# Rotary embedding on one core: the two table loads issued from GpSimd instead of ScalarE

## The chip, the cores and the metric

The kernel runs on one core of one Trainium2 chip. The metric is the device time in microseconds of one execution; lower is better. The profile's span (first to last instruction) is about 2 us shorter than this time.

For a program on one core a timed run is called slow when it lies over 1.5% above the fastest run of its own kernel. Ratios use fast runs only: a ratio is the mean time of one kernel's fast runs over that of the other's of the same rounds, so it is not quite the ratio of the medians quoted.

## The reference

```python
x:   (16, 512, 16, 64) float32      # batch, seq, heads, dim; 33.5 MB
cos, sin: (512, 32) float32         # 64 KB each
x1, x2 = x[..., :32], x[..., 32:]
first  = x1[..., :16] * cos[..., :16] - x1[..., 16:] * sin[..., :16]
second = x1[..., :16] * sin[..., :16] + x1[..., 16:] * cos[..., :16]
return concatenate([first, second, x2], axis=-1)
```

Only the first half of each head is rotated. All of x is read once and written once.

## The kernel before

x is cut into T = 8 tiles of 4 MB, each 128 partitions x 32 KB. A tile is loaded on SyncE's DMA queue, rotated in place on VectorE in two halves, and stored from ScalarE's DMA queue. Five tile buffers exist (`bufs=5`), so the load of tile i+5 waits for the store of tile i.

```python
x_pool  = ...tile_pool(name="xp", bufs=5)
ab_pool = ...tile_pool(name="abp", bufs=1)

stage = const_pool.tile([PB, 2, K, HF], fp32)              # PB = 64 partitions, K = 8, HF = 32
nc.scalar.dma_start(out=stage[:, 0]..., in_=cosf)          # 64 rows of 1 KB
nc.scalar.dma_start(out=stage[:, 1]..., in_=sinf)

table = const_pool.tile([P, 2, K, 2, Q], fp32)
# ... four small VectorE copies, stage -> table (64 partitions to 128) ...

for t in range(T):
    x_t = x_pool.tile([P, K, H, D], fp32)
    nc.sync.dma_start(out=x_t..., in_=xf[t])               # 4 MB, 128 rows of 32 KB
    for k0 in range(0, K, KC):                             # KC = 4: two halves
        # x1, c, s: views of this half of x_t and of the table
        nc.vector.tensor_mul(out=a_t[:], in0=x1, in1=c)
        nc.vector.tensor_mul(out=b_t[:], in0=x1, in1=s)
        nc.vector.tensor_sub(out=x1[:, :, :, 0:Q], in0=..., in1=...)
        nc.vector.tensor_add(out=x1[:, :, :, Q:HF], in0=..., in1=...)
    nc.scalar.dma_start(out=of[t], in_=x_t...)
```

Of the kernel before, what the change touches and what calls it, by code (L numbers as in the profile page):

```python
# [1 line left out]

# [4 lines left out]


@with_exitstack
def kernel(  # L10
    ctx: ExitStack,
    tc: tile.TileContext,
    x: bass.AP,
    cos: bass.AP,
    sin: bass.AP,
    out: bass.AP,
):
    nc = tc.nc
    fp32 = mybir.dt.float32
    P = 128  # L20
    B, S, H, D = x.shape
    Q = D // 4
    HF = D // 2


    K = 8
    T = B * S // (P * K)
    PB = S // K
    REP = P // PB

    xf = x.rearrange("b s h d -> (b s h d)").rearrange("(t p f) -> t p f", t=T, p=P)
    of = out.rearrange("b s h d -> (b s h d)").rearrange("(t p f) -> t p f", t=T, p=P)
    cosf = cos.rearrange("(p k) j -> p (k j)", k=K)
    sinf = sin.rearrange("(p k) j -> p (k j)", k=K)

    const_pool = ctx.enter_context(tc.tile_pool(name="const", bufs=1))
    x_pool = ctx.enter_context(tc.tile_pool(name="xp", bufs=5))
    ab_pool = ctx.enter_context(tc.tile_pool(name="abp", bufs=1))

    stage = const_pool.tile([PB, 2, K, HF], fp32)  # L40
    nc.scalar.dma_start(out=stage[:, 0].rearrange("p k j -> p (k j)"), in_=cosf)  # L41
    nc.scalar.dma_start(out=stage[:, 1].rearrange("p k j -> p (k j)"), in_=sinf)


    table = const_pool.tile([P, 2, K, 2, Q], fp32)
    for r in range(REP):
        for t in range(2):
            nc.vector.tensor_copy(  # L48
                out=table[r * PB : (r + 1) * PB, t],
                in_=stage[:, t, :, 0:Q].unsqueeze(2).to_broadcast((PB, K, 2, Q)),  # L50
            )
    C = table[:, 0].rearrange("p k c j -> p k (c j)")
    Sn = table[:, 1].rearrange("p k c j -> p k (c j)")

    KC = 4
    for t in range(T):
        x_t = x_pool.tile([P, K, H, D], fp32)
        nc.sync.dma_start(out=x_t.rearrange("p k h d -> p (k h d)"), in_=xf[t])  # L58
        for k0 in range(0, K, KC):
            x1 = x_t[:, k0 : k0 + KC, :, 0:HF]  # L60
            c = C[:, k0 : k0 + KC].unsqueeze(2).to_broadcast((P, KC, H, HF))
            s = Sn[:, k0 : k0 + KC].unsqueeze(2).to_broadcast((P, KC, H, HF))
            a_t = ab_pool.tile([P, KC, H, HF], fp32)
            b_t = ab_pool.tile([P, KC, H, HF], fp32)
            nc.vector.tensor_mul(out=a_t[:], in0=x1, in1=c)  # L65
            nc.vector.tensor_mul(out=b_t[:], in0=x1, in1=s)  # L66
            nc.vector.tensor_sub(  # L67
                out=x1[:, :, :, 0:Q], in0=a_t[:, :, :, 0:Q], in1=b_t[:, :, :, Q:HF]
            )
            nc.vector.tensor_add(  # L70
                out=x1[:, :, :, Q:HF], in0=a_t[:, :, :, Q:HF], in1=b_t[:, :, :, 0:Q]
            )
        nc.scalar.dma_start(out=of[t], in_=x_t.rearrange("p k h d -> p (k h d)"))


# [1 line left out]
_INS = ['x', 'cos', 'sin']  # L77
_OUTS = [((16, 512, 16, 64), 'float32')]


# [23 lines left out]
```

## Time and profile before

| | before |
|---|---|
| time, median of 3 runs | 162.37 us (162.19 to 162.39) |
| span of the profiled execution | 160.4 us |
| VectorE (DVE) busy | 110.8 us, 69% |
| DMA engines | full in all but the first and last slices, 419 GB/s over the span |
| first real multiply starts | 18.29 us |

The page of the kernel before. The DMA row gives the mean busy share of the 16 DMA engines in tenths, for 40 equal slices of the span. The queue lines give packets, MB and the share of the 16 engines' time. Group lines end with busy us, mean ns of one, then the idle time just before them and what ended it. Issue lines end with KB each and us from issue to landing.

```profile
DVE 110.8 (69%) x68; POOL 0.2 (0%) x4
...
DMA  7999999999999999999999999999999999999993
GB/s 253 408 400 408 392 417 490 400 408 498 400 400 474 433 392 457 457 392 449 466 392 417 490 400 408 498 400 400 476 425 400 466 441 400 449 457 400 417 482 147
...
q1 hardware_dynamic: 1152, 33.55, 49.3%
q10 hardware_dynamic: 1312, 33.69, 48.7%
...
L65 DVE TENSOR_TENSOR a_t<-x_t,table 128x2048 f32<-128x2048 f32 x16 | 36.7, 2292 | 13.6 <-DMA x_t<-in_x_dram 13.2
...
L48 DVE COPY table<-stage 64x256 f32<-64x256 f32 x4 | 1.1, 287 | 17.1 <-DMA stage<-in_cos_dram 12.2
...
stage<-in_cos_dram ACTq DMA_DIRECT2D x1, 64.0 KB, 11.4
stage<-in_sin_dram ACTq DMA_DIRECT2D x1, 64.0 KB, 16.3
```

From about 4 us on, the DMA engines never rest. q1 is SyncE's queue (x in), q10 ScalarE's (x out and the tables).

The trace also keeps every DMA packet with queue, start, duration and size; the numbers called "packet records" below are counted from those. A 32 KB row of x is one packet of 1.213 us; 16 engines at that pace move 16 x 32768 B / 1.213 us = 432 GB/s. Each engine moves 64 packets in and 64 out: 128 x 1.213 = 155.3 us, and 157.0 us with the slower early loads and the tables. The first packet starts 1.8 us into the span, the last end at 158.2 to 159.2, and the gaps on each engine sum to at most 0.4 us.

The chain of waits of the kernel before, in order of time (start us, us, what):

```profile
1.30 16.34 DMA stage<-in_sin_dram
...
18.29 2.29 DVE a_t L65
...
59.83 34.11 DMA out_dram<-x_t
...
93.99 34.21 DMA x_t<-in_x_dram
...
140.97 1.14 DVEq L99
```

The chain begins with 16 us of waiting for two 64 KB tables. The next pieces show that a load waits for a store that waits its turn in a full queue. The chain names what released what. The last store, issued at 142.1 us, had to queue behind store 6, which landed at 150.0 us (semaphore landings): 7.9 us of slack between VectorE's last result and an engine free to move it.

### The profile page before, as it was taken

The page shows a single profiled execution, that of the slowest core. Times are in us where ns is not written, and L with a number is a line of the kernel's source. Part 1 is how long each engine was busy: PE and PEld are TensorE (multiplying, and loading weights), DVE is VectorE, ACT ScalarE, POOL GpSimd, SP SyncE. Part 2 cuts the span into 40 slices and gives each one's busy share as a digit, 9 for nine tenths or more (in the row PEclk, how much of TensorE's full clock was granted, in tenths as well). Part 3 has the DMA queues.
Part 4 walks back from the last instruction along what each step waited for, and adds up shares of the span by engine and source line. Part 5 has one row for each costly group of instructions (what it writes and reads, how often), then busy time and mean ns, then how long its engine had stood idle before and what let it go on. Part 6 is the DMA issues. An engine that isn't in the chain of part 4 may idle for free.

```text
span 160.4 us, 155 instructions
## 1 busy us (share of the span) xinstructions
DVE 110.8 (69%) x68; POOL 0.2 (0%) x4
## 2 busy tenths in 40 slices
DVE  0001599999999999999998799609995099940000
POOL 0000000000000000000000000000000000000000
DMA  7999999999999999999999999999999999999993
GB/s 253 408 400 408 392 417 490 400 408 498 400 400 474 433 392 457 457 392 449 466 392 417 490 400 408 498 400 400 476 425 400 466 441 400 449 457 400 417 482 147
DMA packets 2465, 67.25 MB, mean 419 GB/s; under 512 B 288, under 2 KB 416, under 8 KB 416
## 3 DMA queue, kind: packets, MB, share of 16 engines
q1 hardware_dynamic: 1152, 33.55, 49.3%
q10 hardware_dynamic: 1312, 33.69, 48.7%
q14 instruction: 1, 0.01, 0.0%
HBM read 33.69 MB, written 33.55 MB: 419 GB/s over the span
## 4 chain that ended last, share of the span: by engine, by line
DMA 53%; DVE 30%; issue 4%; DVEq 1%; ACTq 0%; SPq 0%
DMA x_t<-in_x_dram 21%; DMA out_dram<-x_t 21%; DVE b_t L66 11%; DMA stage<-in_sin_dram 10%; DVE a_t L65 10%; DVE x_t L70 5%; DVE x_t L67 4%; DVEq L99 1%; ACTq L41 0%; DVE table L48 0%; SPq L58 0%; DVEq L65 0%
## 5 line engine op out<-in xcount | busy, mean ns | idle before, releaser
L65 DVE TENSOR_TENSOR a_t<-x_t,table 128x2048 f32<-128x2048 f32 x16 | 36.7, 2292 | 13.6 <-DMA x_t<-in_x_dram 13.2
L66 DVE TENSOR_TENSOR b_t<-x_t,table 128x2048 f32<-128x2048 f32 x16 | 36.5, 2284 | 0.0
L67 DVE TENSOR_TENSOR x_t<-a_t,b_t 128x1024 f32<-128x1024 f32 x16 | 19.6, 1226 | 0.6
L70 DVE TENSOR_TENSOR x_t<-a_t,b_t 128x1024 f32<-128x1024 f32 x16 | 19.5, 1218 | 0.0
L48 DVE COPY table<-stage 64x256 f32<-64x256 f32 x4 | 1.1, 287 | 17.1 <-DMA stage<-in_cos_dram 12.2
L88 POOL MEMSET const-bfloat16-1.0<- 128x1 bf16 x1 | 0.1, 102 | 0.0
L88 POOL MEMSET const-uint8-127<- 128x1 uint8 x1 | 0.1, 102 | 0.0
L88 POOL MEMSET const-float32-0.0<- 128x1 f32 x1 | 0.1, 99 | 0.2 <-issue 0.2
L88 POOL MEMSET const-float32-1.0<- 128x1 f32 x1 | 0.1, 99 | 0.0
## 6 DMA issues: line engine op xcount, KB each, us to landing
x_t<-in_x_dram SPq DMA_DIRECT2D x8, 4096.0 KB, 33.9
out_dram<-x_t ACTq DMA_DIRECT2D x8, 4096.0 KB, 31.3
stage<-in_cos_dram ACTq DMA_DIRECT2D x1, 64.0 KB, 11.4
stage<-in_sin_dram ACTq DMA_DIRECT2D x1, 64.0 KB, 16.3
```

What stands on the lines that cost most here:

```text
L48: nc.vector.tensor_copy(out=table[r * PB : (r + 1) * PB, t], in_=stage[:, t, :, 0:Q].unsqueeze(2).to_broadcast((PB, K, 2, Q)),)
L65: nc.vector.tensor_mul(out=a_t[:], in0=x1, in1=c)
L66: nc.vector.tensor_mul(out=b_t[:], in0=x1, in1=s)
L67: nc.vector.tensor_sub(out=x1[:, :, :, 0:Q], in0=a_t[:, :, :, 0:Q], in1=b_t[:, :, :, Q:HF])
L70: nc.vector.tensor_add(out=x1[:, :, :, Q:HF], in0=a_t[:, :, :, Q:HF], in1=b_t[:, :, :, 0:Q])
L88: nc = _bacc.Bacc("TRN2", target_bir_lowering=False, num_devices=1)
L99: with _tile.TileContext(nc) as tc:
```

## The change

The intent: in the packet records of the kernel before, each 1 KB row of a table is a packet of its own on ScalarE's queue, and an engine alternates it (46 ns) with a 32 KB x packet (1.213 us). From GpSimd's queue several rows were expected to go in one packet (the prediction says why), so the tables should land sooner, and the two other queues are left to x.

```diff
-    nc.scalar.dma_start(out=stage[:, 0].rearrange("p k j -> p (k j)"), in_=cosf)
-    nc.scalar.dma_start(out=stage[:, 1].rearrange("p k j -> p (k j)"), in_=sinf)
+    nc.gpsimd.dma_start(out=stage[:, 0].rearrange("p k j -> p (k j)"), in_=cosf)
+    nc.gpsimd.dma_start(out=stage[:, 1].rearrange("p k j -> p (k j)"), in_=sinf)
```

## The prediction

> **What bounds the kernel now.** The 16 DMA engines, start to end. In the page's 40 slices the DMA share is 9 in all but the first (7) and last (3). In the packet records a 32 KB x packet takes 1.213 us on its engine, and each engine moves 64 in and 64 out: loads 64 x 1.234 (mean), stores 64 x 1.213, table packets 8 x 0.047, together 157.0 us. The first packet starts at 1.8 us, the last end at 158.2 to 159.2, and each engine's gaps add up to at most 0.35 us. The span is 160.4. VectorE is busy 110.8 us (69%).
>
> **What the change moves.** By the instruction order, only the two table loads, from ScalarE's DMA queue to GpSimd's. The fifth x load no longer waits for cos.
>
> Today both tables come as 1 KB packets on ScalarE's queue. In the packet records each engine alternates one of them (46 ns) with one x packet (1.213 us), so ten table packets per engine (eight data, two completion) wait for about ten x packets: the first at 6.0 us; cos lands at 12.2, sin at 17.65. The Trainium skill, "DMA: Bandwidth & Descriptors" ("Queues, rings and completion order"), has the engines go round-robin between queues by packet; the trace agrees. Its section "SWDGE vs HWDGE vs iDMA" prefers packets up to 4096 B for descriptors that GpSimd writes; no run shows that yet. Four 1 KB rows would be one packet, and each table would wait for one or two x packets. Estimate: cos lands at 6 to 9 us, sin at 7 to 11.
>
> **What lies on the path.** The first multiply (18.3 us) waits for sin; x tile 0 landed at 13.6. Its start moves to about 13.2, released by x: 5 us earlier. The first store moves from 32.1 to about 27.
>
> But almost no DMA work goes away: the same bytes cross the same full engines. Stores share the engines with loads earlier, so loads come later. Sharing, a tile in and a tile out take 19.4 us. Loads run alone until 27; 5.4 tiles are left, so the last x tile lands at about 133 (128.2 before). Its 13.9 us of VectorE end at about 147 (142.1 before); store 6 lands at about 148.7 (150.0 before, by the semaphore landings). The last store still queues behind it; slack falls from 7.9 to about 2 us. Total packet time sets the end. Possible gain: some of the 1.4 us by which early x packets exceed 1.213 each (0.6 of it at 8 to 16 us, among table packets). Possible loss: a gap under 1 us before the last store, or GpSimd start and end costs.
>
> **Prediction: 162.1 us, 161.2 to 163.2.** Faster by over 2%: 0.02; within: 0.95; slower: 0.03.
>
> **What would show each step right or wrong.**
> - Queues: a third carries 0.13 MB; tables land under 10 us after issue (11.4 and 16.3 before).
> - Waits: the first multiply is released by x at 13 to 14 us; the 5 us of idle reappear before later multiplies (waits for x 13.2 us before, about 25 after).
> - Chain: last x at about 133, last VectorE work at about 147.
> - DMA share 9 throughout; GB/s within 1% of 419.
>
> **What would make it wrong.** Tables after about 30 us (loads then run dry for want of buffers). The last tile computed over 2 us after store 6. GpSimd's descriptors slowing x packets, or a longer start or end. Load-only and mixed stretches differing in rate (431 against 437 to 443 GB/s by stretch).

## The result, and the profile after

| | before | after |
|---|---|---|
| time, median of 6 runs | 162.28 us (162.16 to 162.77) | 162.56 us (162.36 to 162.86) |
| ratio of fast runs | | 1.0015 (95%: 0.9998 to 1.0033) |
| span of the profiled execution | 160.4 us | 160.6 us |
| cos, sin landed | 12.2, 17.65 us | 8.5, 11.4 us |
| first real multiply | 18.29 us | 13.97 us |
| first store issued | 32.14 us | 27.81 us |
| last x tile landed | 128.2 us | 133.2 us |
| last VectorE result | 142.1 us | 147.1 us |
| store 6 landed | 150.0 us | 150.05 us |

The page of the kernel after, the same lines as above and the new ones:

```profile
DVE 110.8 (69%) x68; POOL 1.4 (1%) x6
...
DMA  7999999999999999999999999999999999999993
GB/s 253 408 392 416 392 465 449 392 392 522 392 392 514 400 392 498 416 392 465 449 392 441 473 392 433 482 392 424 490 386 400 514 392 400 490 416 400 490 416 139
...
q1 hardware_dynamic: 1152, 33.55, 49.3%
q10 hardware_dynamic: 1152, 33.55, 48.4%
q0 software_dynamic: 64, 0.13, 0.2%
...
L65 DVE TENSOR_TENSOR a_t<-x_t,table 128x2048 f32<-128x2048 f32 x16 | 36.7, 2292 | 24.8 <-DMA x_t<-in_x_dram 24.4
...
L48 DVE COPY table<-stage 64x256 f32<-64x256 f32 x4 | 1.1, 288 | 10.9 <-DMA stage<-in_cos_dram 8.5
...
stage<-in_cos_dram POOLq DMA_DIRECT2D x1, 64.0 KB, 7.3
stage<-in_sin_dram POOLq DMA_DIRECT2D x1, 64.0 KB, 9.6
```

A third queue, q0, carries the tables: 64 packets, which the packet records show as 32 of 4096 B and 32 of 4 B, so each engine sees two packets per table where it saw five. The tables land 4 and 7 us sooner after issue. VectorE's idle time before the table copies falls from 17.1 to 10.9 us. The idle time waiting for x, before the multiplies, rises from 13.2 to 24.4 us. VectorE's start is earlier; it waits more later. The DMA row is digit for digit the same.

The chain of waits of the kernel after:

```profile
0.74 13.13 DMA x_t<-in_x_dram
...
13.97 2.29 DVE a_t L65
...
55.50 34.48 DMA out_dram<-x_t
...
90.06 43.09 DMA x_t<-in_x_dram
...
145.91 1.14 DVEq L99
```

The start of the chain is now the first x tile. The saved 4.3 us are gone by the last load: it is issued 3.9 us earlier, takes 43.09 us from issue to landing instead of 34.21, and lands 5.0 us later. Stores began to share the engines earlier; late_tile1 below shows the reverse.

### The profile page after: what moved, and what is told of

Same layout as the page of the kernel before. It is cut to its first block, busy times and chain, and to the rows that moved or that the text cites. A ratio compares the mean times of both kernels' runs of the same rounds, so it can differ in the third digit from the quotient of the medians.

```text
span 160.6 us, 155 instructions
## 1 busy us (share of the span) xinstructions
DVE 110.8 (69%) x68; POOL 1.4 (1%) x6
## 4 chain that ended last, share of the span: by engine, by line
DMA 56%; DVE 31%; issue 3%; DVEq 1%; SPq 0%
DMA x_t<-in_x_dram 35%; DMA out_dram<-x_t 21%; DVE b_t L66 11%; DVE a_t L65 10%; DVE x_t L70 5%; DVE x_t L67 5%; DVEq L99 1%; DVEq L65 0%; SPq L58 0%
## 5 line engine op out<-in xcount | busy, mean ns | idle before, releaser
L65 DVE TENSOR_TENSOR a_t<-x_t,table 128x2048 f32<-128x2048 f32 x16 | 36.7, 2292 | 24.8 <-DMA x_t<-in_x_dram 24.4
L66 DVE TENSOR_TENSOR b_t<-x_t,table 128x2048 f32<-128x2048 f32 x16 | 36.5, 2283 | 0.0
L48 DVE COPY table<-stage 64x256 f32<-64x256 f32 x4 | 1.1, 288 | 10.9 <-DMA stage<-in_cos_dram 8.5
L41 POOL DMA_DIRECT2D stage<-in_cos_dram x1 | 0.7, 651 | 0.8 <-PEq L99 0.8
L42 POOL DMA_DIRECT2D stage<-in_sin_dram x1 | 0.5, 518 | 0.0
```

The costliest lines, as they stand in the source:

```text
L41: nc.gpsimd.dma_start(out=stage[:, 0].rearrange("p k j -> p (k j)"), in_=cosf)
L42: nc.gpsimd.dma_start(out=stage[:, 1].rearrange("p k j -> p (k j)"), in_=sinf)
L48: nc.vector.tensor_copy(out=table[r * PB : (r + 1) * PB, t], in_=stage[:, t, :, 0:Q].unsqueeze(2).to_broadcast((PB, K, 2, Q)),)
```

## The experiments

Theory A is that of the prediction: the 16 DMA engines are full from start to end, so the sum of packet times sets the end, and VectorE's start only moves slack about. The rivals: B, the start is worth its own time and something hid that; C, the early start gains about 4 us and GpSimd's tables cost as much; D, VectorE's share of the chain, or the last tile's compute, sets the end. E and F were formed after the first eight runs. Every batch was timed together with the kernel before on one chip; its median was 162.39 or 162.44 us. The first eight runs used one chip, the last four (held_three, held_six, half_compute_held, extra_1mb) another.

| run | first multiply, us | median, us | ratio to before (95%) |
|---|---|---|---|
| late_tile1 | 24.0 | 162.4 (3 fast of 6 runs) | 0.999 (0.997 to 1.002) |
| late_tile3 | 43.5 | 172.73 | 1.064 (1.061 to 1.066) |
| no_tables (wrong result) | 13.1 | 162.50 | 1.000 (0.998 to 1.002) |
| half_compute (wrong result) | 14.0 | 165.08 | 1.017 (1.014 to 1.020) |
| double_mul_before | 17.95 | 213.14 | 1.312 |
| double_mul_after | 14.18 | 209.13 | 1.288 |
| held_start | 16.5 | 163.71 (1 fast of 6 runs) | none given |
| act_4k_rows (wrong result) | 14.6 | 163.04 | 1.004 (1.003 to 1.005) |
| held_three | 19.1 | 162.50 | 1.001 (1.000 to 1.002) |
| held_six | 23.7 | 164.53 | 1.013 (1.011 to 1.014) |
| half_compute_held (wrong result) | 16.7 | 162.04 | 0.998 (0.997 to 1.000) |
| extra_1mb | 14.1 | 169.84 | 1.047 (1.045 to 1.048) |

### VectorE's start moved far back: late_tile1 and late_tile3

The tables go on SyncE's queue behind two, or four, x tiles (edit against the changed kernel):

```diff
-    nc.gpsimd.dma_start(out=stage[:, 0]..., in_=cosf)
-    nc.gpsimd.dma_start(out=stage[:, 1]..., in_=sinf)
+    early = []
+    for t in range(2):                      # late_tile3: range(4)
+        x_t = x_pool.tile([P, K, H, D], fp32)
+        nc.sync.dma_start(out=x_t..., in_=xf[t])
+        early.append(x_t)
+    nc.sync.dma_start(out=stage[:, 0]..., in_=cosf)
+    nc.sync.dma_start(out=stage[:, 1]..., in_=sinf)
     # ... below, the loop over the tiles takes x_t from early where it can ...
```

> Tables on SyncE's queue behind x tile 1, so VectorE's first multiply should start at about 24 us (14.0 after the change, 18.3 before it). Theory A (the DMA engines are full from start to end, so VectorE's start only moves slack): the time stays at that of before, ratio 0.995 to 1.005, about 162.3 us, with the last store queued behind store 6. Rival B (VectorE's start is worth its own time, and something in the changed kernel hid that): about 5.5 us slower than before, ratio 1.034.

> Tables behind x tile 3: VectorE starts at about 43 us. Theory A: this is beyond the slack. Only five tiles have buffers, so the loads run dry at about 51 us while store 0 can be issued only at 57 (43.3 + 13.9). Estimate by counting packets of 1.213 us, 128 per engine, with VectorE at 13.9 us per tile: the engines stand idle for about 9 us in all, ratio 1.05 to 1.06, about 171 us. Rival B: 25 us slower than before, ratio 1.15.

With the start at 24.0 us, 5.7 us later than before and 10 us later than after, the fast runs take the same time (ratio 0.999). In the profiled one, which is fast, the stores begin later, so the loads have the engines to themselves for longer: the last x tile lands at 124.4 us and VectorE's last result comes at 138.3 us, before the 142.1 us of the kernel before. Three more runs of this kernel took 165.8 to 167.0 us and count as slow. They lie 3.4 to 4.6 us above before, not far below rival B's 5.5 us, so the reading rests on three fast runs and their trace; nothing is concluded from the slow ones, but see held_start below. With the start at 43.5 us the time rises by 10.3 us, close to the 9 us counted in packets and far from the 25 us of rival B. Where it comes from is visible in late_tile3's table of stretches (stretch and its length in us, VectorE busy, GpSimd busy, clock, DMA share, GB/s):

```profile
40.00:52.00 12.00, 8.99 (x9) 0.00 (x0) 1.00 0.96 393
52.00:58.00 6.00, 5.93 (x5) 0.00 (x0) 1.00 0.00 0
58.00:64.00 6.00, 5.96 (x4) 0.00 (x0) 1.00 1.02 437
```

Five tiles are loaded, all buffers are taken, and no store is ready until 57.9 us: the engines stand still for 6 us. By the packet records the idle time adds up to about 8.6 us per engine, some of it at 68 to 70 us, before the loads resume. Only then does VectorE's start cost time. Theory A stands, and B falls.

### The tables taken away: no_tables

```diff
-    nc.gpsimd.dma_start(out=stage[:, 0]..., in_=cosf)
-    nc.gpsimd.dma_start(out=stage[:, 1]..., in_=sinf)
+    nc.vector.memset(stage[:], 1.0)
```

> The changed kernel without its table loads (the tables are filled with 1.0 on VectorE: a wrong result on purpose). First multiply at 13 to 14 us, released by x. Theory A: only the tables' own packet time goes away, 0.4 us per engine, and perhaps the 0.6 us by which x packets run over 1.213 us while tables interleave: 0.3 to 1.0 us faster than before, ratio 0.993 to 0.999. Rival C (issuing from GpSimd costs something at start, end or in x packets that ate a gain of about 4 us): about 4 us faster, ratio 0.975.

The ratio is 1.0002: rival C's 4 us are not there. GpSimd's table loads, in sum, cost nothing that five rounds can see. The small gain of 0.3 to 1.0 us that was expected did not show either. In the profiled execution the x packets do lose their early slow stretch (packets up to 1.5 us while tables interleave: 8 to 16 us before, 4 to 10 us after, absent here), but about 1.2 us per engine of slow packets appear later, most of them at 28 to 33 us, where stores begin. One profiled execution is not enough to call that a trade.

### Half the compute: half_compute

```diff
-        for k0 in range(0, K, KC):
+        for k0 in range(0, KC, KC):
```

> The changed kernel with only the first half of each tile rotated (a wrong result on purpose): VectorE's busy time falls from 110.8 to about 56 us. The chain of waits gives VectorE 31% of the span. Theory A: no change, ratio 0.995 to 1.003; the time VectorE spends is slack. Rival D (the last tile's compute and store, or the chain's VectorE share, set the end): at least the last tile's 6.9 us faster, ratio 0.957 or less.

Rival D falls as it was stated: taking away half of VectorE's work gains nothing. But Theory A fails here as well: the kernel is 1.7% slower, by fast runs alone. Its profiled execution fell in the slow state (170.7 us), so it can suggest a cause, but not show that of the fast runs. Its DMA row and two stretches:

```profile
DMA  7999999999999999999999999999999999940983
...
148.00:150.00 2.00, 1.18 (x1) 0.00 (x0) 1.00 0.61 262
150.00:155.00 5.00, 4.97 (x4) 0.00 (x0) 1.00 0.11 46
```

In this execution the engines do stand idle, about 6 us each between 149 and 157 us. The last x tile landed only at 148.7 us, because a few engines were behind: most had moved their last load packet by 140 us, the slowest at 147.2. Store 6 landed at 158.45 us, but most engines were done with it by 150, while VectorE was still at work on the last tile. So here the last tile's compute and store do end up on the path. Packets that took longer make up the rest, about 1.8 us per engine. Its packet order is taken up below.

### VectorE made the limit: double_mul_before and double_mul_after

In each of the two kernels the two multiplies are written twice in a row, with the same result:

```diff
             nc.vector.tensor_mul(out=a_t[:], in0=x1, in1=c)
             nc.vector.tensor_mul(out=b_t[:], in0=x1, in1=s)
+            nc.vector.tensor_mul(out=a_t[:], in0=x1, in1=c)
+            nc.vector.tensor_mul(out=b_t[:], in0=x1, in1=s)
```

> The kernel before with each of its two multiplies done twice (same result): VectorE needs about 23.0 us per tile instead of 13.9, 184 us in all, more than the 157 us of the DMA engines. Theory A: now VectorE sets the time: its start at 18.3, 8 x 23.0 of work, then one store of about 10 to 12 us: span about 213, time about 215 us.

> The changed kernel with the multiplies doubled in the same way. Theory A: where VectorE is the limit, its earlier start (14.0 against 18.3) is worth its whole 4.3 us: about 211 us against double_mul_before, so 2% faster than that kernel. Rival C (GpSimd's tables cost about as much as the earlier start gives): no difference from double_mul_before.

Two lines from the order of time (start us, us, engine, line, operation, idle before), first from double_mul_before, then from double_mul_after:

```profile
17.95 2.29 DVE L65 TENSOR_TENSOR a_t<-x_t,table 128x2048 f32<-128x2048 f32 x1
```

```profile
14.18 2.29 DVE L65 TENSOR_TENSOR a_t<-x_t,table 128x2048 f32<-128x2048 f32 x1 [1.93 <-DMA x_t<-in_x_dram]
```

The start is 3.8 us earlier, and the time is 213.14 - 209.13 = 4.0 us shorter, 1.9%. The same edit that is worth nothing in the kernel at hand is worth its whole head start when VectorE is busy almost without a break (86 and 87% of the span in these two). Rival C falls a second time. Both absolute times came out about 2 us under the estimates.

### Who issues, or how many packets: act_4k_rows

ScalarE issues again, but 16 rows of 4 KB per table. The rows land in partitions the kernel does not need them in. Its output is wrong, which doesn't matter for the time.

```diff
-    nc.gpsimd.dma_start(out=stage[:, 0]..., in_=cosf)
-    nc.gpsimd.dma_start(out=stage[:, 1]..., in_=sinf)
+    stage4 = const_pool.tile([16, 2, 1024], fp32)
+    nc.scalar.dma_start(out=stage4[:, 0], in_=cos.rearrange("(p k) j -> p (k j)", k=32))
+    nc.scalar.dma_start(out=stage4[:, 1], in_=sin.rearrange("(p k) j -> p (k j)", k=32))
+    # stage is filled with 1.0, then its first 16 partitions from stage4
```

> Tables from ScalarE's queue again, but as 16 rows of 4 KB instead of 64 of 1 KB (a wrong result on purpose: the rows land in other partitions than the kernel needs). If the number of packets per engine sets the landing, whoever issues them: two packets per table and engine, cos lands at about 8.5 us and sin at about 11 us, as from GpSimd. If it is GpSimd's own queue that brings them early: cos at about 12, sin at about 17 as before. Time in both cases as before, ratio 0.995 to 1.003.

The DMA issues of act_4k_rows:

```profile
stage<-in_cos_dram ACTq DMA_DIRECT2D x1, 64.0 KB, 5.8
stage<-in_sin_dram ACTq DMA_DIRECT2D x1, 64.0 KB, 8.5
```

The tables land 5.8 and 8.5 us after issue, even sooner than from GpSimd (7.3 and 9.6). So fewer packets per engine are enough to bring the tables early, and GpSimd is not needed for it: 1 KB rows from ScalarE took 11.4 and 16.3. The time is 0.4% above before, just outside the expected band; no cause of that was tested.

### GpSimd's tables with a held start, and what half_compute ran into: held_start, held_three, held_six, half_compute_held

In the changed kernel, filler multiplies that nothing reads are put on VectorE after the table copies: two in held_start, three in held_three, six in held_six; half_compute_held is half_compute with two.

```diff
+    hold = const_pool.tile([P, 2048], fp32)
+    for _ in range(2):                      # held_three: 3, held_six: 6
+        nc.vector.tensor_mul(out=hold..., in0=table[:, 0]..., in1=table[:, 1]...)
     C = table[:, 0]...
```

> The changed kernel with two filler multiplies on VectorE after the table copies, so that its first real multiply starts at about 16.5 to 18 us, as before the change, while the tables still come from GpSimd. Theory A: ratio to before 0.997 to 1.003. Rival C (an early start gains, GpSimd's tables lose): slower than before by what the early start had hidden, 2 to 4 us, ratio 1.012 or more.

Its one fast run, the profiled one, took 163.71 us, 0.8% above before and outside Theory A's band; five more took 167.7 to 169.7 us and count as slow by the distance from that one. Taken alone this looks a little like rival C. But VectorE's start is only half of what changed: the fillers also move the moment at which the stores join the loads. From the packet records one can count how many load packets per engine are ahead when the first store packet starts, and how many x packets after the first 20 us took over 1.3 us instead of 1.213:

| kernel (profiled execution) | lead, packets per engine | into a tile of 8 | packets over 1.3 us, of about 1800 |
|---|---|---|---|
| before | 27.0 | 3.0 | 1 |
| after | 23.2 | 7.2 | 6 |
| act_4k_rows | 23.8 | 7.8 | 1 |
| no_tables | 23.75 | 7.75 | 32 |
| held_start (span 161.9) | 25.6 | 1.6 | 80 |
| half_compute (a slow execution) | 17.9 | 1.9 | 105 |
| held_three | 27.9 | 3.9 | 13 |
| half_compute_held | 20.0 | 4.0 | 3 |
| held_six | 33.0 | 1.0 | 47 |
| late_tile1 (fast; 3 of its 6 runs were slow) | 32.0 | 0.0 | 26 |

The first six rows led to Theory E, before the last three kernels ran: a lead of 1 to 2 packets into a tile slows the mixed loads and stores, and otherwise Theory A holds. (Late_tile1 had run by then too; its row was added afterwards.) Rival F: the fillers, or the later start, cost the time.

> held_start and half_compute came out slower than Theory A said. In their packet records x packets take over 1.3 us again and again, unevenly over the engines, and at the first store the loads are 25.6 and 17.9 packets per engine ahead: 1.6 and 1.9 packets into a tile. In the kernels that ran at 162.4 us this lead is 27.0 (before: 3.0 into a tile), 23.2 (after: 7.2) and 23.75 (without tables: 7.75). Theory E (a lead of 1 to 2 packets into a tile slows the mixed loads and stores; otherwise Theory A holds): a third filler multiply moves the lead to about 27.4, 3.4 into a tile, so this kernel, which starts later than held_start, is faster than it: ratio to before 0.997 to 1.006. Rival F (the fillers or the later start cost the time): at least as slow as held_start, 167 us or more.

> The same with six fillers. VectorE's first real store comes about 9.2 us later than in held_start, close to one tile of loading (9.7 us), so the lead should be about 33, again 1 to 2 into a tile. Theory E: slow again, ratio 1.015 or more, with x packets over 1.3 us throughout the mixed stretch. Theory A alone (slack lasts to a start of about 30 us): ratio 0.997 to 1.005. Rival F: slower than held_start.

> half_compute with the two fillers of held_start: the first store comes 2.5 us later, the lead moves from 17.9 to about 20 packets, 3.8 to 4 into a tile. Theory E: the loss of half_compute goes away, ratio 0.995 to 1.005, which is also what Theory A had said of half the VectorE work. Rival (half the compute itself costs time, through earlier stores): as slow as half_compute, ratio about 1.017.

With one filler more held_three is back at ratio 1.001, with GpSimd's tables and a start at 19.1 us. Rivals C and F fall. half_compute_held is at 0.998. These lines of its page show what Theory A had said of half the compute from the start, VectorE busy for 60.5 us (fillers included) instead of 110.8 and the engines full in all but the first and last slices:

```profile
DVE 60.5 (38%) x38; POOL 1.4 (1%) x6
...
DMA  6999999999999999999999999999999999999995
```

held_six slows again, by 1.3% with all runs fast, a little less than expected. But its slow packets are not spread over the whole mixed stretch, as the expectation had it: 37 of the 47 lie between 64 and 78 us. Its trace offers another cause. Load 5 needs the buffer of tile 0, and is issued only here (start us, us, engine, line, operation):

```profile
62.84 0.33 SPq L65 DMA_DIRECT2D x_t<-in_x_dram  x1
```

Store 0 landed at 62.75 us, and tile 4, the last one with a buffer, at 62.56. From 59.8 to 67.5 us no load packet starts; in the kernel before, the longest such gap is 3.0 us. The long packets come when the loads resume, as they do after the standstill of late_tile3 (38 packets over 1.3 us at 70 to 76 us). Five buffers hold 40 packets per engine and a store takes 8, so, as an estimate, a lead over 32 empties the load queue before store 0 is done; late_tile1, at 32.0, has a gap of 4.5 us and its fast runs lose nothing. held_six is therefore no clean test of Theory E.

What is shown: the moment at which the stores join the loads matters. On one chip and in fast runs alone, held_three (first store packet at 36.5 us) takes the time of before and held_six (43.4 us) takes 1.3% more. What is not shown: that the position inside a tile decides. A plainer reading was not tested: too late a first store leaves the loads without buffers (held_six), too early a one brings the last tile late (half_compute, 24.3 us), and all between costs nothing. Against it stands held_start alone (33.7 us), with 0.8% in its single fast run and the 80 long packets of that run. The rule "1 to 2 packets into a tile" fits all ten rows, but six of them made it, and held_start and half_compute ran on another chip than the two kernels in which a filler is said to remove their loss; neither was run again there. (The kernel before took the same time on both chips.) The mechanism (which memory or port the two streams meet in) was not tested and stays open.

### More traffic: extra_1mb

```diff
         nc.sync.dma_start(out=x_t..., in_=xf[t])
+        if t == 4:
+            spare = const_pool.tile([64, 4096], fp32)
+            nc.sync.dma_start(out=spare[:], in_=xf[0, 0:64, 0:4096])
```

> The changed kernel with one load more, 1 MB of x in rows of 16 KB into a spare tile behind x tile 4, which nothing reads (four packets of 0.61 us per engine). Theory A: 2.4 us slower, ratio about 1.015, because every byte waits in the same full queues. If the last tile's compute or some other slack could hide traffic: no change. The four short packets let the stores catch up by two large ones, so the lead goes from 7.2 to about 5 into a tile, clear of 1 to 2 by Theory E.

It cost 7.5 us, three times as much as expected. The table of stretches of extra_1mb shows where the rest is:

```profile
140.00:150.00 10.00, 7.18 (x5) 0.00 (x0) 1.00 1.00 433
150.00:156.00 6.00, 5.96 (x4) 0.00 (x0) 1.00 0.33 142
156.00:168.00 12.00, 0.56 (x1) 0.00 (x0) 1.00 0.82 350
```

In packet records each engine is idle for 4.0 to 5.6 us, at this place. The four half-size load packets of each engine took turns with store packets, so they gave about four whole turns to the stores, and no x load packet started from 71.8 to 83.0 us. The loads fell back: the last x tile landed at 142.7 us instead of 133.2, and VectorE's last result came at 156.6. The slack left by the change, 150.05 - 147.1 = 3.0 us, was used up, and the engines ran dry. The sum for the profiled execution, per engine: 2.9 us for the spare packets (0.73 us each on average, where 0.61 was expected), 0.8 us by which x packets took longer, and 4.4 us more idle time than before make 8.1 us; this execution took 170.45 us, 8.1 above before, and the median is 7.5 above. The expected size was wrong mainly because the delay of the last tile was left out; the view that the end comes when the engines have moved every packet, plus the time they stand idle, holds.

## Why the prediction was right

- **What bounds the kernel.** Right. The DMA row is the same before and after. Moving VectorE's start from 14.0 to 19.1 and 24.0 us (held_three; fast runs of late_tile1) leaves the time within 0.2% of before, and half the compute leaves it there too in half_compute_held, though not in half_compute (1.7% slower). At 43.5 us, once the engines stand idle, the time rises by 10.3 us.
- **Tables land sooner.** Right: cos at 8.5 (6 to 9 estimated), sin at 11.4 (7 to 11, slightly late). The reason given, fewer packets per engine, is shown by act_4k_rows.
- **The head start.** Right: the first multiply at 13.97 us (about 13.2), released by x. VectorE's waits for x became 24.4 us (about 25).
- **Where the gain went.** Right: into slack at the end. The last x tile landed at 133.2 us (133), VectorE ended at 147.1 (147), store 6 landed at 150.05 (148.7), so the slack fell from 7.9 to 3.0 us (about 2). double_mul shows that the 4 us are real where there is no such slack.
- **The possible gain.** Did not come: the slow early x packets were not removed, they moved from 8 to 16 us to 4 to 10 us, and they amount to 1.4 us per engine in both kernels. The time stayed at 162.56 us, where 162.1 was predicted, inside the range.
- **Left out.** The prediction took the end to depend on total packet time and on the last tile being ready in time (it named that risk: "The last tile computed over 2 us after store 6"). It did not see that the moment at which stores join the loads can change both: 1.3% in fast runs of held_six, 1.7% in those of half_compute. Packets took about 1.1 us more per engine in held_start and 1.4 us more in held_six; in half_compute's slow execution the engines also ran dry before the last store. The change moved that moment by 4.8 us and met neither loss (31.2 us, 7.2 packets into a tile). Nothing in the prediction says why it should not have, so in this respect it was lucky. Had it cost 1 to 2%, blaming GpSimd for it would have been wrong.

## What to carry to other kernels

Before making something start earlier, look whether the busiest unit is ever idle because of it: if the DMA engines are full from the first microsecond to the last, an earlier start only turns into a longer wait elsewhere, and the chain of waits will not tell you so. To get a small load through beside a large stream, count packets per engine, not bytes: here each 1 KB packet waited for about one of 32 KB. When an experiment moves the phase of two streams against each other, shift it once more by a packet or two before you believe a difference of 1 to 2%.

## What the Trainium skill lacked or had wrong

- "DMA: Bandwidth & Descriptors", section "Queues, rings and completion order", has the engines go round-robin by packet; the trace agrees (one 46 ns table packet, one 1.213 us x packet, in turn). It gives a typical packet as 9 to 17 descriptors. In this profile's records (whether they mean by a packet what the page does is not shown) every 32 KB and every 1 KB row from SyncE and ScalarE is a packet of its own; only GpSimd's rows were joined, four of 1 KB into one of 4096 B, as the section "SWDGE vs HWDGE vs iDMA" would have it. The consequence for a small load beside a large one (11.4 and 16.3 us to land 64 KB, against 5.8 and 8.5 with 4 KB rows from the same queue) is not there.
- The same page's section "Where 436 GB/s comes from" says that for HBM to SBUF transfers the HBM side, about 358 GB/s, binds. Read alone, that misleads here: with one core running, the kernel before moved 431 GB/s while it only loaded (18 to 36 us) and 419 GB/s over its whole span, loads and stores together; the same passage's 435 GB/s fabric ceiling fits, as does the 425 GB/s that it quotes for a measurement of 16 MB.
- The same page, "Rules for kernel authors", says that spreading DMAs over issuing engines does not help bandwidth; nothing here is against it (419 GB/s in both kernels), but only 0.13 of 67 MB changed the queue.
- No page says that the moment at which a store stream joins a load stream of equal packets can cost time: 1.3% in held_six, none that shows (1.001) in held_three, whose first store packet comes 6.9 us earlier on the same chip.
